# Column differences of the up weights: three units in four made ahead, the fourth made from its own loads

## The chip, the cores and the metric

The kernel runs on one core of a Trainium2 chip. The metric is the device time of one execution in microseconds; "before" is the median of three runs. Engines are named as in the profile: PE is TensorE's matmuls and PEld its weight loads, DVE is VectorE, ACT is ScalarE, POOL is GpSimd, SP is SyncE, which here does nothing but issue DMAs.

## The reference

One layer of a transformer block on x of 512 rows and 2048 columns, float32 throughout:

```python
h = rmsnorm(x, g_attn)
proj = h @ w_in                      # 2048 x 6152: q, k, v of 8 + 8 heads of 128, and 8 forget gates
o_sb = stick_breaking_attention(...) # 8 heads
o_fox = forgetting_attention(...)    # 8 heads
x = x + concat(head_rmsnorm(o_sb), head_rmsnorm(o_fox)) @ w_out
u = relu(rmsnorm(x, g_mlp) @ w_up)   # w_up: 2048 x 8192
x = x + (u * u) @ w_down             # w_down: 8192 x 2048
return rmsnorm(x, g_final)
```

## The kernel before

**Precision.** A float32 operand is split into a high part, cast on ACT (L63), and a low part, which DVE subtracts (L64). A plain product is then three matmuls (`mm3`, L95). The split tiles are `wh`, `wl` from a pool with three places each, and every fourth pair of the up stage comes from one more place and is called `wx`.

**Stages.** First the input projection and the attention of 16 heads (0 to some 590 us), then the output projection (to some 820 us), then the up product (to some 1477 us), then the down product, then the end. The change touches the first and the third.

**The up product** (class `Unit`). The 8192 columns of w_up are done in 32 units of 256 columns. Each unit is a 2 x 2 block product with seven products instead of eight: the rows of w_up in two interleaved halves, the columns in two blocks of 128, so a unit has blocks b11, b12, b21, b22 of 1024 x 128, 512 KB each. The seven products need, beside b11, b21 and b22, the differences

```
S1 = b12 - b11      product 5      (t1)
S3 = b22 - b12      product 7      (t3)
S2 = b22 - S1       product 6      (t2)
S4 = b21 - S2       product 4      made in the unit, L674
```

The sums of the rows' side (`F`, tiles `fh1` to `fh7` and `fl1` to `fl7`) are made once. A unit has three places of `rw` (five places of 8 KB per partition in all): one for b11 and t2, one for t1 and t3, one for b21 and b22, which come as one load of 1 MB (L646). Product p of the program order 1, (4 of the unit before), 5, 6, (3 of the unit before), 2, 7 takes 8 full-width matmuls with the high part (L678) and 8 half-width ones with the low part (L680). Products 1, 6, 7, 4 of a unit add up in one psum bank `psa`; ACT copies it out after 1, 6 and 7 as `s1`, `s6`, `s7` (L684), and each copy has to be done before the next of these products may write the bank. Products 5 and 3 use `psc`, product 2 `psb`.

**Stores between.** When a pair of units is done, the seven row-side sums of its 512 hidden columns are made for the down product (`store_form`, L708): DVE adds, ACT and DVE split into a tile `st`, and SP stores it in `ufd` in DRAM (L713). `st` has three places (tag `wraw`), so the cast of a set's fourth tile waits for the first store, and so on: the seventh waits for the fourth.

**Early sums.** S1, S3 and, for even units, S2 are made long before, among the projections of the first stage: `load_sums` reads b11, b12, b22 (three loads of 512 KB, L153) into a place that x used, two places in turn; DVE subtracts in place (L161, L162, L164); SP stores the result in `td` (L166). Odd units have only S1 and S3 made early, and make S2 in the unit, `b[6] = b[3] - b[5]` (L671), from b22 and S1. `drip` calls this along with the weight loads of `project_q`, 64 in number: at call n the sets up to 32 (n - 4) / 58 are done, each with the loads of the next set ahead of it.

**Order.** The order of each engine comes from a scheduler that runs its own timeline when the kernel is built; only PE's order in the first stage is written by hand. `tc.issue_after(i)` keeps what it covers behind instruction i. SP issues in its order: a DMA that waits for a place or for data holds all behind it.

## Time and profile before

| | |
|---|---|
| median of three runs | 2104.38 us (2103.6 to 2106.39) |
| the profiled execution | 2103.3 us, its span 2101.5 us |
| granted TensorE clock, mean | 0.995 |
| busy: PE, DVE, ACT | 98%, 76%, 51% of the span |
| moved by DMA | 464 MB, 221 GB/s |

The span is what the profiler saw from the first instruction to the last. Busy times of engines overlap, so they don't add up to the span. In the views below a row names the line, the engine, the operation and the tiles written and read (out<-in, numbers left out), and an arrow in brackets gives the idle time just before a row and what ended it. Rows of a timeline start with the time from the span's start and the duration. In windows each engine has its busy time and, in brackets, its instructions; then come the granted clock, the DMA engines' share and GB/s.

### The profile page before, as it was taken

How to read it: one execution, taken by the hardware profiler on the slowest of the kernel's cores; microseconds unless marked ns; L12 is line 12 of the kernel's file. 1: busy time of each engine (PE TensorE's matmuls, PEld its weight loads, DVE VectorE, ACT ScalarE, POOL GpSimd, SP SyncE). 2: the span in 40 equal slices, each digit the busy share in tenths (PEclk: the TensorE clock that was granted, in tenths of full speed). 3: DMA queues.
4: the chain of work that ended last, by engine and by line, in shares of the span. 5: the costliest groups of instructions: out<-in, count | busy, mean ns of one | idle time of the engine just before them, and what ended most of it. 6: DMA issues, size and time to landing. Idle time of an engine off the chain costs nothing.

```text
span 2101.5 us, 26836 instructions
## 1 busy us (share of the span) xinstructions
PE 2063.8 (98%) x10292; PEld 1753.2 (83%) x10292; DVE 1606.8 (76%) x1827; ACT 1064.9 (51%) x1426; POOL 64.9 (3%) x77
## 2 busy tenths in 40 slices
PE   9999999999999999999999999999999999999998
PEld 8888888888798888888888888888788888888886
DVE  5647757758766567777887888788788988988886
ACT  6334434444455565665665666566644444433433
POOL 0000000000110000000000000000000000000003
PEclk9999999999999999999999999999999999999999
DMA  7848958949963445566677576768867665764732
GB/s 240 288 120 265 325 171 292 347 118 293 316 211 110 151 140 171 187 229 236 228 243 237 198 247 230 240 209 275 314 203 260 240 223 177 261 235 145 259 122 80
DMA packets 358880, 464.27 MB, mean 221 GB/s; under 512 B 11696, under 2 KB 255456, under 8 KB 348640
## 3 DMA queue, kind: packets, MB, share of 16 engines
q1 hardware_dynamic: 357792, 460.44, 65.8%
q10 hardware_dynamic: 960, 2.13, 0.3%
q8 instruction: 81, 1.33, 0.2%
q14 instruction: 47, 0.39, 0.1%
HBM read 351.37 MB, written 111.15 MB: 220 GB/s over the span
## 4 chain that ended last, share of the span: by engine, by line
PE 81%; DMA 8%; DVE 5%; ACT 3%; issue 2%; SPq 0%; DVEq 0%; ACTq 0%
PE accd L96 8%; PE accd L98 8%; PE accd L97 8%; PE psa L678 7%; DMA ufd<-st 5%; PE accq L96 5%; PE accq L98 5%; PE accq L97 5%; PE psa L680 3%; PE psc L678 3%; PE acco L97 3%; PE acco L98 3%; PE acco L96 3%; PE accv L96 3%; PE accv L97 3%; PE accv L98 3%
## 5 line engine op out<-in xcount | busy, mean ns | idle before, releaser
L63 ACT CAST wh<-wraw 128x1024 fp32r<-128x1024 f32 (+2 forms) x133 | 135.4, 1019 | 178.8 <-PE accq L97 103.7
L63 ACT CAST wh<-wd 128x1024 fp32r<-128x1024 f32 (+1 forms) x136 | 135.0, 1000 | 178.9 <-PE accd L98 118.9
L64 DVE TENSOR_TENSOR wl<-wraw,wh 128x1024 fp32r<-128x1024 f32 (+2 forms) x133 | 158.0, 1188 | 75.9 <-ACT wh L63 75.6
L64 DVE TENSOR_TENSOR wl<-wu,wh 128x1024 fp32r<-128x1024 f32 x166 | 202.0, 1221 | 9.1 <-ACT wh L63 6.1
L96 PE MATMUL accq<-hH,wh 128*128 128x512 f32 x512 | 201.3, 393 | 0.0
L98 PE MATMUL accq<-hH,wl 128*128 128x512 f32 x512 | 200.1, 391 | 0.0
L97 PE MATMUL accq<-hL,wh 128*128 128x512 f32 x512 | 199.6, 390 | 0.0
L63 ACT CAST wh<-wu 128x1024 fp32r<-128x1024 f32 x166 | 172.1, 1047 | 46.1 <-issue 18.5
L64 DVE TENSOR_TENSOR wl<-wd,wh 128x1024 fp32r<-128x1024 f32 (+1 forms) x136 | 155.5, 1154 | 41.1 <-ACT wh L63 40.9
L96 PE MATMUL accd<-wh,uf 128*128 128x512 f32 x436 | 169.8, 389 | 2.6 <-DVE c L701 1.7
L98 PE MATMUL accd<-wh,uf 128*128 128x512 f32 x436 | 169.6, 389 | 0.0
L97 PE MATMUL accd<-wl,uf 128*128 128x512 f32 x436 | 169.6, 389 | 0.0
L63 ACT CAST wx<-wd 128x1024 fp32r<-128x1024 f32 (+1 forms) x88 | 87.5, 1000 | 123.1 <-PE accd L98 79.5
L678 PE MATMUL psa<-fh,wh 128*128 128x512 f32 x388 | 107.5, 399 | 14.2 <-ACT s L684 14.2
L64 DVE TENSOR_TENSOR wx<-wd,wx 128x1024 fp32r<-128x1024 f32 (+1 forms) x88 | 100.9, 1154 | 22.5 <-ACT wx L63 22.4
L98 PEld LDWEIGHTS accq<-hH,wl 128*128 128x128 f32 x512 | 96.1, 188 | 20.2
L97 PEld LDWEIGHTS accq<-hL,wh 128*128 128x128 f32 x512 | 96.4, 188 | 19.2
L96 PEld LDWEIGHTS accq<-hH,wh 128*128 128x128 f32 x512 | 96.4, 188 | 18.9
L96 PE MATMUL accd<-wx,uf 128*128 128x512 f32 x284 | 110.4, 389 | 0.1
L779 DVE TENSOR_TENSOR m<-m,accd 128x1024 f32<-128x1024 f32 x84 | 102.2, 1217 | 10.9 <-PE accd L98 10.8
L97 PE MATMUL accd<-wx,uf 128*128 128x512 f32 x284 | 110.5, 389 | 0.0
L98 PE MATMUL accd<-wx,uf 128*128 128x512 f32 x284 | 110.5, 389 | 0.0
(286 smaller groups left out, 4884.3 us busy)
## 6 DMA issues: line engine op xcount, KB each, us to landing
ufd<-st SPq DMA_DIRECT2D x98, 512.0 KB, 5.4
sums<-in_w_up_dram SPq DMA_DIRECT2D x96, 512.0 KB, 6.5
wd<-in_w_down_dram SPq DMA_DIRECT2D x48, 1024.0 KB, 6.8
wraw<-in_w_in_dram SPq DMA_DIRECT2D x84, 512.0 KB, 6.1
uf<-ufd SPq DMA_DIRECT2D x42, 1024.0 KB, 7.2
wu<-td SPq DMA_DIRECT2D x79, 512.0 KB, 5.0
wu<-in_w_up_dram SPq DMA_DIRECT2D x32, 1024.0 KB, 8.1
td<-sums SPq DMA_DIRECT2D x16, 1536.0 KB, 8.3
```

The source lines that it names most:

```text
L63: ins = casts[0] = act.copy(hi, src)
L64: lows[0] = dve.tensor_tensor(lo, src, hi.bitcast(F32), op=ALU.subtract)
L96: pe.matmul(out, sh, mh, start=first, stop=False, skip_group_check=True)
L97: pe.matmul(out, sh, ml, start=False, stop=False, skip_group_check=True)
L98: pe.matmul(out, sl, mh, start=False, stop=last, skip_group_check=True)
L678: pe.matmul(ps, hi[:, a, :], both, start=a == 0 and p in (1, 2, 5), stop=False, skip_group_check=True)
L680: pe.matmul(ps[:, :2 * P], lo[:, a, :], F[p][a // 4][:, a % 4, 0, :], start=False, stop=a == KC // 2 - 1, skip_group_check=True)
L779: dve.tensor_tensor(M[p][:, :, db, :], M[p][:, :, db, :], ps, op=ALU.add)
```

## The change

1. Units with u % 4 != 3 (24 of 32) get all three differences early, one set of three subtractions each, stored as one DMA. The odd units among them no longer make S2 themselves.
2. Units with u % 4 == 3 (8) get none early. They load b12 once and b22 twice more (L659 to L661: t1, t3, t2) and make S3 and S1 ahead of product 5 (L677, L678) and S2 ahead of product 6 (L680), all on DVE.
3. `drip` is written anew: at call n, 4n - 20 is divided by 9, and a remainder under 4 makes the set of that number, so a set every 2.25 calls. The loads of set i + 2 go out two calls after the store of set i, behind the weight load of that call. The first two sets' loads go out at call 2.

```diff
--- before.py
+++ after.py
@@ -56,7 +56,7 @@
     acc_cm = tc.tile_pool(name="acc", bufs=4, space=PSUM)
     acc = acc_cm.__enter__()
 
-    lows, casts = [None], [None]
+    lows, casts, loads = [None], [None], [None]
 
     def split(hi, lo, src, scale=None):
         if scale is None:
@@ -83,7 +83,7 @@
         src = src if isinstance(src, list) else [src]
         for i, r in enumerate(src):
             n = b // len(src)
-            sp.dma_start(raw[:, :, i * n:(i + 1) * n], r)
+            loads[0] = sp.dma_start(raw[:, :, i * n:(i + 1) * n], r)
         out = []
         per = min(a, 2 * NT // b)
         for i in range(0, a, per):
@@ -146,36 +146,36 @@
     td = [dp.tile([P, 3, KC // 2, P], F32, name=f"td{u}") for u in range(NU)]
     up_rows = w_up.rearrange("(a i p) f -> i p a f", i=2, p=P)
 
-    def load_sums(u):
-
-        r = mixp.tile([P, 3, KC // 2, P], F32, tag=f"x{u % 2}", name="sums")
+    def load_sums(u, i):
+
+        r = mixp.tile([P, 3, KC // 2, P], F32, tag=f"x{i % 2}", name="sums")
         for j, (i, c) in enumerate(((0, 2 * u), (0, 2 * u + 1), (1, 2 * u + 1))):
             sp.dma_start(r[:, j], up_rows[i][:, :, c * P:(c + 1) * P])
         return r
 
-    def up_sums():
-        r = load_sums(0)
-        for u in range(NU):
-            b11, b12, b22 = (r[:, j] for j in range(3))
-            now, r = r, load_sums(u + 1) if u + 1 < NU else None
+    early = [u for u in range(NU) if u % 4 != 3]
+    drops, raws, waiting = [0], {}, []
+
+    def drip(low, load):
+
+        drops[0] += 1
+        i, j = divmod(drops[0] * 4 - 20, 9)
+        with tc.issue_after(load.ins):
+            if drops[0] == 2:
+                raws.update((k, load_sums(early[k], k)) for k in range(2))
+            if waiting and (waiting[0][0] <= drops[0] or (j < 4 and waiting[0][1] == i)):
+                k = waiting.pop(0)[1]
+                raws[k] = load_sums(early[k], k)
+        if j > 3 or not 0 <= i < len(early):
+            return
+        b11, b12, b22 = (raws[i][:, j] for j in range(3))
+        with tc.issue_after(low.ins):
             dve.tensor_tensor(b11, b12, b11, op=ALU.subtract)
             dve.tensor_tensor(b12, b22, b12, op=ALU.subtract)
-            if u % 2 == 0:
-                dve.tensor_tensor(b22, b22, b11, op=ALU.subtract)
-            n = 2 if u % 2 else 3
-            yield sp.dma_start(td[u][:, :n], now[:, :n])
-
-    sums = up_sums()
-    drops = [0, 0]
-
-    def drip(ins):
-
-        drops[0] += 1
-        while drops[1] < min(NU, NU * (drops[0] - 4) // 58):
-            drops[1] += 1
-            with tc.issue_after(ins.ins):
-                next(sums)
-
+            dve.tensor_tensor(b22, b22, b11, op=ALU.subtract)
+        sp.dma_start(td[early[i]], raws.pop(i))
+        if i + 2 < len(early):
+            waiting.append((drops[0] + 2, i + 2))
 
     with (
         tc.tile_pool(name="hp", bufs=1) as hp,
@@ -260,7 +260,7 @@
             step = 8
             for k0 in range(0, KC, step):
                 w = load_w(w_in[k0 * P:(k0 + step) * P, c0:c0 + P].rearrange("(a p) c -> p a c", p=P), step, P)
-                drip(lows[0])
+                drip(lows[0], loads[0])
                 for i in range(step):
                     k = k0 + i
                     mm3(ps, *w[i], hH[:, k, :], hL[:, k, :], k == 0, k == KC - 1)
@@ -654,8 +654,14 @@
                 r, q = blocks(), blocks()
                 b11, t2, t1, t3 = r[:, 0], r[:, 1], q[:, 0], q[:, 1]
             sp.dma_start(b11, first[:, :, :P])
-            for t_, j in ((t1, 0), (t3, 1)) if u % 2 else ((t1, 0), (t2, 2), (t3, 1)):
-                sp.dma_start(t_, td[u][:, j])
+            self.raw = u not in early
+            if self.raw:
+                sp.dma_start(t1, first[:, :, P:])
+                sp.dma_start(t3, last[:, :, P:])
+                sp.dma_start(t2, last[:, :, P:])
+            else:
+                for t_, j in ((t1, 0), (t2, 2), (t3, 1)):
+                    sp.dma_start(t_, td[u][:, j])
             b21, b22 = wide(last)
             self.b = {1: b11, 5: t1, 6: t2, 2: b21, 7: t3, 3: b22, 4: b21}
             self.A, self.B, self.C = (ups.tile([P, NT], F32, tag=c, name=f"ps{c}") for c in "abc")
@@ -667,8 +673,11 @@
                 self.pair = hidden[0]
                 self.c = hidden[0][:, self.u % 2]
             hi, lo = (w.rearrange("p (a b) -> p a b", b=P) for w in hi_lo(2 * NT))
-            if p == 6 and self.u % 2:
-                dve.tensor_tensor(self.b[6], self.b[3], self.b[5], op=ALU.subtract)
+            if p == 5 and self.raw:
+                dve.tensor_tensor(self.b[7], self.b[7], self.b[5], op=ALU.subtract)
+                dve.tensor_tensor(self.b[5], self.b[5], self.b[1], op=ALU.subtract)
+            if p == 6 and self.raw:
+                dve.tensor_tensor(self.b[6], self.b[6], self.b[5], op=ALU.subtract)
             split(hi, lo, self.b[p])
             if p == 2:
                 dve.tensor_tensor(self.b[4], self.b[2], self.b[6], op=ALU.subtract)
```

What stands in the engines' order at the hand-over from unit 19 to unit 20, before and after. First SP's queue. The tiles `wu` are places of the units' operands, `td20` and `td21` the stored differences of units 20 and 21, `ufd` the stores of one set, the fourth of which is ufd6. Before:

```order
L713 DMA ufd1_14_6909<-st_10320 256x1x512
L713 DMA ufd4_14_6912<-st_10380 256x1x512
L658 DMA wu_10533<-td20_130 128x1024 x2
L713 DMA ufd5_14_6913<-st_10425 256x1x512
L646 DMA wu_10538<-in_w_up_dram 128x8x256
L656 DMA wu_10714<-in_w_up_dram 128x8x128
L713 DMA ufd6_14_6914<-st_10477 256x1x512
L713 DMA ufd2_14_6910<-st_10505 256x1x512
L713 DMA ufd7_14_6915<-st_10565 256x1x512
L713 DMA ufd3_14_6911<-st_10612 256x1x512
L658 DMA wu_10715<-td21_131 128x1024 x2
```

and now:

```order
L664 DMA wu_10500<-td20_130 128x1024 x2
L722 DMA ufd5_14_6865<-st_10392 256x1x512
L646 DMA wu_10505<-in_w_up_dram 128x8x256
L656 DMA wu_10681<-in_w_up_dram 128x8x128
L664 DMA wu_10681<-td21_131 128x1024
L722 DMA ufd6_14_6866<-st_10444 256x1x512
L722 DMA ufd2_14_6862<-st_10472 256x1x512
L722 DMA ufd7_14_6867<-st_10532 256x1x512
L664 DMA wu_10682<-td21_131 128x1024 x2
L722 DMA ufd3_14_6863<-st_10579 256x1x512
```

One more block, of td21, is read ahead of the fourth store (ufd6), and unit 21's other two now stand ahead of the seventh store (ufd3) and not behind it; one row carries both. In the pair before, unit 19's own t1 and t3 (L659, L660) stand at the place of that row, and its t2 (L661) at that of the single block.

Second ACT's order at the same place. `s6` and `s7` are the copies of unit 19's bank, `st` the casts of a set (the last one is the seventh), `c` the squares of relu; before:

```order
L63 CAST st_10477<-c_9931 128x512
L63 CAST st_10505<-c_9931 128x512
L63 CAST wh_10543<-wu_10532 128x1024
L684 COPY s6_10451<-psa_10355 128x512
L63 CAST st_10565<-c_9931 128x512
L63 CAST wh_10570<-wu_10353 128x1024
L63 CAST wh_10592<-wu_10533 128x1024
L705 ACTIVATE c_10297<-c_10297 128x1024
L63 CAST st_10612<-c_9931 128x512
L63 CAST wx_10617<-wu_10532 128x1024
L706 ACTIVATE c_10297<-c_10297 128x1024
L684 COPY s7_10528<-psa_10355 128x512
```

and now:

```order
L63 CAST st_10444<-c_9895 128x512
L63 CAST st_10472<-c_9895 128x512
L63 CAST st_10532<-c_9895 128x512
L63 CAST wh_10537<-wu_10318 128x1024
L63 CAST wh_10559<-wu_10500 128x1024
L693 COPY s6_10418<-psa_10320 128x512
L714 ACTIVATE c_10261<-c_10261 128x1024
L63 CAST wh_10605<-wu_10318 128x1024
L715 ACTIVATE c_10261<-c_10261 128x1024
L63 CAST st_10579<-c_9895 128x512
L63 CAST wh_10630<-wu_10505 128x1024
L693 COPY s7_10495<-psa_10320 128x512
```

The sixth cast moved ahead of s6, the seventh stands behind unit 19's product 3 (wh_10605), and between it and s7 there is now only the cast of unit 20's product 2 (wh_10630).

Third PE's order there. psa_10355 and psa_10320 are unit 19's bank before and now, psa_10540 and psa_10507 unit 20's; the digit of fh and fl is the number of the product. Before, from the middle of unit 19's product 7:

```order
L678 MATMUL psa_10355<-fl7_5711,wx_10509 128x512 x4
L680 MATMUL psa_10355<-fh7_5710,wx_10509 128x256 x4
L680 MATMUL psa_10355<-fl7_5711,wx_10509 128x256 x4
L678 MATMUL psa_10540<-fh1_5698,wh_10543 128x512 x4
L678 MATMUL psa_10540<-fl1_5699,wh_10543 128x512 x4
L680 MATMUL psa_10540<-fh1_5698,wl_10544 128x256 x4
L680 MATMUL psa_10540<-fl1_5699,wl_10544 128x256 x4
L678 MATMUL psc_10542<-fh5_5706,wh_10592 128x512 x4
L678 MATMUL psc_10542<-fl5_5707,wh_10592 128x512 x4
L680 MATMUL psc_10542<-fh5_5706,wl_10593 128x256 x4
L680 MATMUL psc_10542<-fl5_5707,wl_10593 128x256 x4
L678 MATMUL psa_10355<-fh4_5704,wh_10570 128x512 x4
```

and now, from unit 20's product 5:

```order
L687 MATMUL psc_10509<-fh5_5658,wh_10559 128x512 x4
L687 MATMUL psc_10509<-fl5_5659,wh_10559 128x512 x4
L687 MATMUL psa_10320<-fh7_5662,wx_10476 128x512 x4
L687 MATMUL psa_10320<-fl7_5663,wx_10476 128x512 x4
L689 MATMUL psa_10320<-fh7_5662,wx_10476 128x256 x4
L689 MATMUL psa_10320<-fl7_5663,wx_10476 128x256 x4
L689 MATMUL psc_10509<-fh5_5658,wl_10560 128x256 x4
L689 MATMUL psc_10509<-fl5_5659,wl_10560 128x256 x4
L687 MATMUL psb_10508<-fh2_5652,wh_10630 128x512 x4
L687 MATMUL psb_10508<-fl2_5653,wh_10630 128x512 x4
L687 MATMUL psa_10320<-fh4_5656,wh_10537 128x512 x4
L687 MATMUL psa_10320<-fl4_5657,wh_10537 128x512 x4
```

Unit 19's product 7 moved behind unit 20's product 1 and the high part of its product 5, and the high part of unit 20's product 2 moved ahead of unit 19's product 4.

## The prediction

> **What bounds the kernel now.** The page comes first, then the waits of PE, then PE in order of time, and then the engines around its longest stops. In the page's first part the columns are busy time, share and instructions; in the waits they are the total in us, how often, and the longest.
>
> ```profile
> span 2101.5 us, 26836 instructions
> PE 2063.8 (98%) x10292; PEld 1753.2 (83%) x10292; DVE 1606.8 (76%) x1827; ACT 1064.9 (51%) x1426; POOL 64.9 (3%) x77
> ...
> PE psa L678 <- ACT s L684: 15.3, 11, 3.4
> PE s L96 <- DVE pl L64: 3.1, 1, 3.1
> ```
>
> TensorE sets the time: only 38 us of the span are not matmuls. The matmuls stay as they are, so the change can win only from stops of PE, and lose only by new ones. Four tenths of the idle time is one kind: the up product's matmuls wait for ScalarE's copy of a psum bank. How long should that stage be? The pace of an undisturbed unit and the stage's first and last starts tell.
>
> ```profile
> 1238.95 1.10 PE L678 MATMUL psb<-fh,wh 128*128 128x512 f32 x4
> 1258.51 1.09 PE L678 MATMUL psb<-fh,wh 128*128 128x512 f32 x4
> ...
> L678 PE MATMUL psa<-fh,wh x388: 389/395/628, 819.5 to 1471.7; 128*128 128x512 f32 x194
> L678 PE MATMUL psc<-fl,wx x68: 388/389/395, 851.1 to 1475.5; 128*128 128x512 f32 x68
> ```
>
> Both psb rows are product 2, of units 20 and 21; between them lie the seven products of a unit: 19.56 us, 2.79 us each. 32 units make 625.9 us. The stage takes from 819.5 to about 1476.8 (the last start and the 1.3 us of low-half matmuls behind it), 657.3 us. So some 31 us are lost in it, of which I count the first 20 us and the hand-over at the end out: neither changes. Five stops carry most of the rest; the bracket is the idle time before the row.
>
> ```profile
> 983.09 1.35 PE L678 MATMUL psa<-fh,wh 128*128 128x512 f32 x4 [2.62 <-ACT s L684]
> 1065.00 1.34 PE L678 MATMUL psa<-fh,wh 128*128 128x512 f32 x4 [1.93 <-ACT s L684]
> 1310.18 1.19 PE L678 MATMUL psa<-fh,wh 128*128 128x512 f32 x4 [1.25 <-ACT s L684]
> 1392.64 1.32 PE L678 MATMUL psa<-fh,wh 128*128 128x512 f32 x4 [3.05 <-ACT s L684]
> ```
>
> With the one below they stand 82 us apart or a multiple of it: four units. Each falls where a unit u with u % 4 == 3 hands over to the next. This is the one at unit 19, all engines:
>
> ```profile
> 1214.01 0.38 SPq L646 DMA_DIRECT2D wu<-in_w_up_dram  x1
> 1215.15 0.38 SPq L656 DMA_DIRECT2D wu<-in_w_up_dram  x1
> 1215.75 12.03 SPq L713 DMA_DIRECT2D ufd<-st  x4
> 1225.90 0.62 ACT L63 CAST st<-c 128x512 fp32r<-128x512 f32 x1 [4.07 <-DMA ufd<-st]
> 1226.43 1.04 ACT L63 CAST wx<-wu 128x1024 fp32r<-128x1024 f32 x1
> 1228.33 0.56 ACT L684 COPY s<-psa 128x512 f32<-128x512 f32 x1
> 1228.95 1.44 PE L678 MATMUL psa<-fh,wh 128*128 128x512 f32 x4 [3.43 <-ACT s L684]
> 1233.40 1.08 PE L678 MATMUL psc<-fh,wh 128*128 128x512 f32 x4
> ```
>
> Read it upwards. PE stops because the copy s7 of unit 19 is late; s7 is late because the cast of the seventh store tile (1225.90) stands ahead of it in ScalarE's order and waits for the place that the fourth store frees. That store was issued at 1215.75 and landed 10 us later, behind 1.5 MB of loads issued just before it (unit 20's 1 MB, unit 21's first block). The whole chain from the cast to PE is 3.05 us.
>
> A stop costs more than its length. The product at 1228.95 takes 4.45 us to 1233.40 where 2.79 is normal: 1.66 us more. The windows' granted clock (the number ahead of the last two) says why:
>
> ```profile
> 985.00:988.00 3.00, 3.00 (x14) 2.64 (x12) 2.92 (x4) 1.72 (x3) 0.00 (x0) 0.60 0.53 128
> 1067.00:1070.00 3.00, 3.00 (x14) 2.71 (x13) 2.92 (x4) 1.72 (x3) 0.00 (x0) 0.62 0.53 134
> 1231.00:1234.00 3.00, 3.00 (x14) 2.69 (x13) 2.91 (x4) 1.69 (x3) 0.00 (x0) 0.64 0.56 142
> ```
>
> After the stops of 2.62, 1.93 and 3.43 us the clock was cut to some 0.6 on average over 3 us; I take the same 1.66 us behind 3.05, and none behind 1.25, whose first row (1.19) is nearly normal. So the five stops cost 12.3 us idle and 4 x 1.66 = 6.6 us of slow clock: 18.9 us. [...]
>
> Why is VectorE, and with it the load at 1214.01, so late there? Of the waits between 860 and 1480:
>
> ```profile
> ACT st L63 <- DMA ufd<-st: 60.3, 29, 4.2
> DVE wu L671 <- DMA wu<-in_w_up_dram: 57.8, 15, 5.7
> ...
> 1197.39 1.23 DVE L671 TENSOR_TENSOR wu<-wu 128x1024 f32<-128x1024 f32 x1 [5.71 <-DMA wu<-in_w_up_dram]
> ```
>
> In each odd unit L671 waits at the head of VectorE for the unit's 1 MB load, the last of its loads; all casts' low halves and sums queue behind it, and the loads that need their places.
>
> **The change part by part.** *L671 goes.* Units with u % 4 == 1 get the third difference ready made; their 57.8/15 = 3.85 us waits and one subtraction go. In u % 4 == 3 three subtractions on raw blocks replace the one:
>
> ```profile
> L674 DVE TENSOR_TENSOR wu<-wu 128x1024 f32<-128x1024 f32 x32 | 39.1, 1222 | 0.5
> ...
> 860.00:1480.00 620.00, 603.02 (x3396) 527.66 (x3395) 505.67 (x639) 381.03 (x501) 0.00 (x0) 0.99 0.70 235
> wu<-td SPq DMA_DIRECT2D x79, 512.0 KB, 5.0
> wu<-in_w_up_dram SPq DMA_DIRECT2D x31, 512.0 KB, 8.0
> ```
>
> A subtraction is 1.22 us. In the stage that is 8 x 2 more and 8 x 1 fewer, +9.8 us of VectorE, which is busy 505.7 of 620: hidden by the 57.8 us of waiting that go. The loads grow by one 512 KB block in each odd unit, 16 x 0.52 = 8.4 MB; at 235 GB/s for a share of 0.70, so 336 GB/s at full share, 1.56 us each, 25 us in all, and the share goes to about 0.74: hidden, but for the store behind such a block.
>
> *The long stops.* At unit 19 VectorE gains 5.71 us of wait and pays two subtractions, 2.44: it is 3.3 us ahead, and so is the 1 MB load, since its place comes free with the low half of unit 19's product 7. Ahead of the fourth store stands one more block, +1.56. So that store lands about 1.7 us sooner, near 1224.1 instead of 1225.8. What is needed also moves: by PE's order the products that it runs before it depends on the seventh cast are the same, only unit 19's product 7 now comes behind unit 20's first two, so it comes there again at 1225.5; but what it needs then is one cast of unit 20's product 2 behind the seventh, not two other instructions and s7: 0.62 + 1.04 less their overlap, 1.6 us instead of 3.05. The cast must start by 1223.9; it would by 1224.1. The stop of 3.43 us shrinks to a few tenths, too short for the clock. Over the eight such units I leave 0.4 us each, 3 us: this term is -16. Its bounds are -18.9 and, if the store is as late as now, 0.
>
> *The other stops* of that kind are 15.3 - 12.3 = 3.0 us, several of them behind L671; half goes, -1.5 (0 to -3).
>
> *The early stage.* Of 80 subtractions 8 go, of 96 loads 24, and a set's loads follow two weight loads later, after the store, not at the next set. Before, the queue stood in such loads:
>
> ```profile
> SPq L153 <- DMA td<-sums: 50.0, 19, 5.6
> ...
> 526.98 1.23 DVE L161 TENSOR_TENSOR sums<-sums 128x1024 f32<-128x1024 f32 x1 [1.16 <-DMA sums<-in_w_up_dram]
> 528.12 1.48 DVE L64 TENSOR_TENSOR pl<-pt,ph 128x1280 fp32r<-128x1280 f32 x1
> 529.66 0.53 PE L96 MATMUL s<-uh 128*128 128x512 f32 x1 [3.09 <-DVE pl L64]
> 520.00:540.00 20.00, 16.91 (x81) 14.33 (x80) 12.78 (x12) 8.84 (x10) 0.27 (x2) 0.91 1.06 350
> ```
>
> PE had only this one stop: pl stood behind subtractions, one of which waited 1.16 us for its load while the DMA share was 1.06. Their number ahead of pl is the same in the new order; the wait should go. Of 3.09 us and the 1.66 of the clock (0.91 over 20 us) I take -2.5; bounds 0 and -4.75. The 50 us of the queue gave PE nothing to wait for, so their end gives nothing.
>
> *What the new order of PE costs.* Some copies get less time: between product 6 and 7 of units 4k PE now has only 13 half-width matmuls for a copy of 0.56 us: a product's 2.79 us are eight full and eight half-width ones, so 2.79/24 = 0.116 each, 1.5 us. ScalarE has to be free then. No row shows this; from nothing to 0.8 us (a copy and half a cast late) at eight places, 0 to +6; I take +2, nearer to nothing since the copy fits nearly three times.
>
> Sum: -16 - 1.5 - 2.5 + 2 = -18. The profiled execution's 2103.3 becomes 2085.3; it stands 1.1 below the median of the three runs, so 2086.4, and I say 2086.
>
> **The rivals.** *A new wait at the raw subtraction, slower.* Unit 19's t1 and t3 are now read from the weights, and L677 and L678 need both; then follows the cast.
>
> ```profile
> 1186.93 0.83 SPq L658 DMA_DIRECT2D wu<-td  x2
> 1196.25 1.05 ACT L63 CAST wx<-wu 128x1024 fp32r<-128x1024 f32 x1 [2.46 <-issue]
> 1201.60 1.09 PE L678 MATMUL psc<-fh,wx 128*128 128x512 f32 x4
> ```
>
> Before they were issued at 1186.93 and landed 5.0 us later by the median, 1192. With the five VectorE instructions from L677 to L678 (5.6 us) and the cast's 1.05, product 5 could start at 1198.6, and PE wants it at 1201.6: 2.9 us of cover. But 512 KB from the weights took 8.0 us by the median where a block of td took 5.0, which would use the cover up just so. For it: that row. Against: the 8.0 belongs to loads behind a 1 MB load, and these two now stand behind stores. If they land 2.5 us beyond the cover, every fourth unit stops for 2.5 and pays 1.66: 8 x 4.16 = 33 us, on top of 2086 without the 3 that were left and the 2 of the copies: 2114. It decides from 23 us in all, 2.9 us at each place; a stop of 1.9 us, the shortest behind which the clock was cut, costs 3.6 with it.
>
> *The stop stays.* If L677 holds VectorE as long as L671 did, the 1 MB load is no sooner, and the fourth store is later by 1.56, which the shorter chain (1.4 us) just pays for. Then only the other stops and the early stage give: -4 + 2, 2102.
>
> *Half of it.* The store is only 1 us sooner: half of the 16 goes, 2094.
>
> [...]
>
> **How the numbers follow.** Forecast 0.62 (2086, its own range 2077 to 2092); half 0.10; the clock's other cause 0.02; the stop stays 0.13; the new wait 0.13. Below lie all bounds at their best, -18.9 - 3 - 4.75, 2077.7, so the range begins at 2076; it ends at 2104 with the stop that stays, and leaves out the new wait and a little more. 0.2% is 4.2 us, about what a measurement of this kernel can tell: faster holds the first three, 0.74; the stop that stays is within it, 0.13; slower 0.13.
>
> **What would show it.** Right: no wait of VectorE at the head of odd units beyond 1 us; no PE stop over 1.5 us between 900 and 1460, and windows there with a clock of 1.00; the seventh cast of a set waiting less than 1 us in units 4k; no stop near 529. Wrong: waits of DVE at L677 for DMA of over 3 us, PE stops every 78 us at product 5 or 2, or copies at product 6 of units 4k with stops of their own.

## The result and the profile after

The changed kernel takes 2080.44 us (median of four runs, 2078.39 to 2082.58) where the kernel before took 2103.99 beside it (2102.92 to 2106.39): a ratio of 0.9887, 95% interval 0.9869 to 0.9904. The forecast was 2086, in a range from 2076 to 2104. The profiled execution took 2080.91 us against 2103.3, so it stands for the medians.

The page of the changed kernel, its busy engines and the waits of PE in a view of their own (total us, how often, longest):

```profile
span 2079.2 us, 26762 instructions
PE 2055.9 (99%) x10292; PEld 1747.6 (84%) x10292; DVE 1601.8 (77%) x1827; ACT 1072.2 (52%) x1426; POOL 57.0 (3%) x77
```

```profile
PE accd L96 <- DVE c L710: 2.2, 1, 2.2
PE psa L687 <- DVE fl L64: 1.8, 1, 1.8
PE psa L687 <- ACT s L693: 1.6, 2, 1.4
PE s L96 <- DVE pl L64: 1.0, 1, 1.0
```

PE's waits for the copy out of `psa` have gone from 15.3 us in eleven places to 1.6 in two, and none of these lies before 1400 us. The wait of `accd` at the hand-over to the down stage has grown to 2.2 us, from 1.7 (its row of before is shown with the last unit, below). The up stage itself, the group with its first matmul (816.0 us),

```profile
L687 PE MATMUL psa<-fh,wh x388: 389/395/496, 816.0 to 1447.0; 128*128 128x512 f32 x194
```

and its last matmuls in order of time:

```profile
1451.89 0.64 PE L689 MATMUL psc<-fl,wx 128*128 128x256 f32 x4
```

It runs from 816.0 to 1452.5, 636.5 us instead of 657.3, and it starts 3.5 us sooner. A window over its middle shows the same. Its columns are the busy times of PE, PEld, DVE, ACT and POOL with their instructions, then the granted clock, the DMA share and GB/s; before first:

```profile
860.00:1440.00 580.00, 564.70 (x3182) 494.41 (x3181) 469.37 (x594) 355.60 (x467) 0.00 (x0) 0.99 0.70 232
```

```profile
860.00:1440.00 580.00, 579.11 (x3315) 509.57 (x3314) 495.43 (x631) 378.09 (x487) 0.00 (x0) 1.00 0.77 255
```

PE is busy for 579.1 of 580 us, at the full clock. VectorE (495.4 us for 469.4) and the DMA engines (a share of 0.77 for 0.70) are busier than before and, by these numbers, still have room. The account, by the profiled executions: early stage -3.5, up stage -20.8, everything behind it +2.0, in all -22.3 of the 22.4 by which the two differ.

The stop that the prediction read in detail was that at unit 19, 3.43 us. The same place after the change:

```profile
1194.29 0.38 SPq L646 DMA_DIRECT2D wu<-in_w_up_dram  x1
...
1199.77 0.38 SPq L656 DMA_DIRECT2D wu<-in_w_up_dram  x1
1200.21 0.57 SPq L664 DMA_DIRECT2D wu<-td  x1
1200.87 2.14 SPq L722 DMA_DIRECT2D ufd<-st  x3
1207.61 0.62 ACT L63 CAST st<-c 128x512 fp32r<-128x512 f32 x1 [1.35 <-DMA ufd<-st]
1208.14 1.05 ACT L63 CAST wh<-wu 128x1024 fp32r<-128x1024 f32 x1
1210.51 1.09 PE L687 MATMUL psb<-fh,wh 128*128 128x512 f32 x4
```

The 1 MB load (L646) is issued 6.6 us ahead of the fourth store (the first of the three at 1200.87); before it was 1.74 us. The store lands 6.7 us behind its issue, where it took 10.1. The seventh cast still waits for it, but 1.35 us, and the cast that PE needs behind it ends at 1209.2, 1.3 us before PE wants it (1210.51, no bracket, so no idle time). This cover differs from one execution to the next: in a second profile of the same kernel ("changed, again" below) the cast is late here, and PE stops:

```profile
1211.01 0.50 PE L687 MATMUL psb<-fh,wh 128*128 128x512 f32 x1 [1.16 <-ACT wh L63]
```

The waits of the stage between 860 and 1460 show the rival's place as well:

```profile
ACT st L63 <- DMA ufd<-st: 50.2, 23, 3.9
DVE wu L677 <- DMA wu<-in_w_up_dram: 5.8, 7, 1.7
```

The new head of VectorE in units 4k + 3 waits 1.7 us at most and 5.8 in all, where L671 waited 57.8. ScalarE's casts wait almost as much for stores as before (50.2 us for 60.3), but PE stops behind casts for 0.6 us in all.

### The profile page after: what moved, and what is told of

It reads as the page before. It is cut to its first block, busy times and chain, and to the rows that moved or that the text cites. A ratio compares the mean times of both kernels' runs of the same rounds, so it can differ in the third digit from the quotient of the medians.

```text
span 2079.2 us, 26762 instructions
## 1 busy us (share of the span) xinstructions
PE 2055.9 (99%) x10292; PEld 1747.6 (84%) x10292; DVE 1601.8 (77%) x1827; ACT 1072.2 (52%) x1426; POOL 57.0 (3%) x77
## 4 chain that ended last, share of the span: by engine, by line
PE 83%; DVE 7%; DMA 6%; issue 3%; ACT 1%; SPq 0%; DVEq 0%; ACTq 0%
PE accd L96 8%; PE accd L97 8%; PE accd L98 8%; PE psa L687 7%; PE accq L96 5%; PE accq L98 5%; PE accq L97 5%; PE psa L689 4%; PE psc L687 3%; DMA wu<-in_w_up_dram 3%; PE acco L97 3%; PE acco L98 3%; PE acco L96 3%; PE accv L96 3%; PE accv L97 2%
## 5 line engine op out<-in xcount | busy, mean ns | idle before, releaser
L687 PE MATMUL psa<-fl,wh 128*128 128x512 f32 x388 | 105.9, 391 | 1.8 <-DVE fl L64 1.8
```

What stands on the lines that cost most here:

```text
L687: pe.matmul(ps, hi[:, a, :], both, start=a == 0 and p in (1, 2, 5), stop=False, skip_group_check=True)
```

## The experiments

Each kernel was timed in the same sitting as the kernel before; the ratio is to that. All compute the whole output. "Up stage" is the span of its matmuls in the profile, "idle" a stop of PE in it.

| run | us | ratio, 95% interval | up stage, start and length |
|---|---|---|---|
| before | | | 819.5, 657.3 |
| changed | 2080.4 | 0.9887, 0.9869 to 0.9904 | 816.0, 636.5 |
| e1 loads only | 2106.6 | 1.0022, 1.0011 to 1.0032 | 822.1, 658.1 |
| e2 units only | 2082.0 | 0.9902, 0.9888 to 0.9917 | 817.1, 634.6 |
| e3 wait in 3 mod 4 | 2088.1 | 0.9929, 0.9914 to 0.9944 | 818.8, 643.9 |
| e4 wait in 1 mod 4 | 2086.3 | 0.9921, 0.9907 to 0.9936 | 813.8, 645.3 |
| e5 all early | 2082.8 | 0.9898, 0.9882 to 0.9914 | 823.4, 633.3 |
| e7 store, other queue | 2095.4 | 0.9949, 0.9931 to 0.9967 | 820.0, 652.7 |
| e8 all raw | 2126.0 | 1.0099, 1.0080 to 1.0118 | 814.8, 681.3 |
| e9 store ahead of load | 2084.6 | 0.9919, 0.9904 to 0.9933 | 821.4, 635.6 |
| e10 28 early | 2082.5 | 0.9908, 0.9893 to 0.9923 | 818.2, 638.5 |
| e6 last unit early | 2077.8 | 0.9872, 0.9856 to 0.9888 | 816.3, 635.9 |
| e6, again | 2076.3 | 0.9878, 0.9863 to 0.9893 | 816.4, 633.2 |
| changed, again | 2082.4 | 0.9908, 0.9891 to 0.9924 | 816.0, 638.5 |

**Which half of the change does it.** The change has two halves, where the early loads stand and which unit gets what. One kernel has only the first, one only the second.

Only the loads (base: changed):

```diff
-    early = [u for u in range(NU) if u % 4 != 3]
+    early = list(range(NU))
-        i, j = divmod(drops[0] * 4 - 20, 9)
+        i, j = divmod(drops[0] * 4 - 20, 7)
...
-            dve.tensor_tensor(b22, b22, b11, op=ALU.subtract)
+            if i % 2 == 0:
+                dve.tensor_tensor(b22, b22, b11, op=ALU.subtract)
...
+            if p == 6 and self.u % 2:
+                dve.tensor_tensor(self.b[6], self.b[3], self.b[5], op=ALU.subtract)
```

> Only the loads of the early sums are set as in the changed kernel; the units keep the old distribution (all 32 get sums early, odd units make the third difference in the up stage, behind their 1 MB load). Theory (the 1 MB load that VectorE waits for in odd units makes the fourth store late): the up stage keeps its long stops every fourth unit, 10 to 15 us idle and the slow clock behind each; only the early stop of 3.09 us goes: about 2100 us. Rival (it is where the early loads stand, or the new order that comes of it, that removed the stops): about 2082 us, the up stage as short as in the changed kernel, 636 us. If the early stop stays too, 2104.

Only the units (base: changed, with the loads and the stores of the sums placed as before):

```diff
+        r = load_sums(0)
+        for u in range(NE):
+            b11, b12, b22 = (r[:, j] for j in range(3))
+            now, r = r, load_sums(u + 1) if u + 1 < NE else None
...
+        while drops[1] < min(NE, NE * (drops[0] - 4) // 58):
```

> Only the distribution over the units is as in the changed kernel (24 units with three early differences, eight that subtract their own loads); the early loads stay where they were, each set's behind the sums of the set before. Theory: the up stage as short as in the changed kernel, 636 us instead of 657, and the early stop stays or changes by itself: 2080 to 2084 us. Rival (the position of the early loads did it): about 2100.

The first took 2106.6 us, a little slower than before; the second 2082.0, as the changed kernel. So the units carry it, and where the early loads stand gains nothing. I had put the early stop down to the loads, and that was wrong. The stop in the kernel with the loads alone, and in the one with the units alone:

```profile
528.86 1.23 DVE L174 TENSOR_TENSOR sums<-sums 128x1024 f32<-128x1024 f32 x1 [0.42 <-DMA sums<-in_w_up_dram]
530.00 1.48 DVE L64 TENSOR_TENSOR pl<-pt,ph 128x1280 fp32r<-128x1280 f32 x1
...
531.54 0.50 PE L96 MATMUL s<-uh 128*128 128x512 f32 x1 [3.12 <-DVE pl L64]
```

```profile
528.16 0.50 PE L96 MATMUL s<-uh 128*128 128x512 f32 x1 [1.04 <-DVE pl L64]
```

With the new loads and 32 sets pl is as late as ever (3.12 us); with the old loads and 24 sets the stop is 1.04 us, as it is in the changed kernel. The number of sets alone doesn't decide either. The next kernel, e3, also has 32 sets and the new loads, and there the wait for pl is short:

```profile
PE ssq L325 <- DVE pl L64: 0.5, 1, 0.5
```

In it no subtraction of the sums stands among the three VectorE instructions just ahead of pl; in the kernel with the loads alone two of the three just ahead are such subtractions, both waiting for their loads (0.26 and 0.42 us). So the stop goes by what the order puts ahead of pl, which comes out differently in each kernel.

**Which wait.** The change takes VectorE's wait for the 1 MB load out of two kinds of odd units. Two kernels put it back into one kind each, a third takes it out without any raw unit. All are the changed kernel with these edits.

Back in units 3 modulo 4 (32 sets, no raw unit):

```diff
-            dve.tensor_tensor(b22, b22, b11, op=ALU.subtract)
+            if early[i] % 4 != 3:
+                dve.tensor_tensor(b22, b22, b11, op=ALU.subtract)
...
+            if p == 6 and self.u % 4 == 3:
+                dve.tensor_tensor(self.b[6], self.b[3], self.b[5], op=ALU.subtract)
```

> The changed kernel, except that the units whose number is 3 modulo 4 again get two early differences and make the third behind their 1 MB load, as before; the units 1 modulo 4 keep all three early. Theory (the wait of VectorE in just these units delays the load and so the fourth store): the long stops come back, idle 8 to 12 us in four or five places with the slow clock behind them: 2093 to 2099 us. Rival (the order that comes with 24 early sets, or the waits in the other odd units, held the stops): they stay away, 2078 to 2084.

Back in units 1 modulo 4 (24 sets, units 3 modulo 4 raw):

```diff
-            dve.tensor_tensor(b22, b22, b11, op=ALU.subtract)
+            if early[i] % 4 != 1:
+                dve.tensor_tensor(b22, b22, b11, op=ALU.subtract)
...
+            if p == 6 and self.u % 4 == 1:
+                dve.tensor_tensor(self.b[6], self.b[3], self.b[5], op=ALU.subtract)
```

> The changed kernel, except that the units whose number is 1 modulo 4 get two early differences and make the third behind their 1 MB load; the units 3 modulo 4 subtract their own loads as in the changed kernel. Theory: no long stop comes back, only the short ones of these units, 0 to 3 us: 2080 to 2084 us. Rival (any such wait at the head of VectorE delays stores enough): long stops, 2090 or more.

All 32 early with three sums each:

```diff
-    early = [u for u in range(NU) if u % 4 != 3]
+    early = list(range(NU))
-        i, j = divmod(drops[0] * 4 - 20, 9)
+        i, j = divmod(drops[0] * 4 - 20, 7)
```

> All 32 units get their three differences early; no unit subtracts in the up stage but for the fourth block, and none waits for its 1 MB load there. Theory (that wait alone made the stops; the raw units are needed only to save early work): the up stage as short as in the changed kernel, 634 to 638 us, the early stage 0 to 6 us longer for its 8 more sets: 2080 to 2086 us. Rival (the raw units bring the gain by their own loads, which relieve the store queue): stops come back at every fourth unit, 2090 or more.

The last is the clearest. PE does not stop at all in its window:

```profile
860.00:1440.00 580.00, 580.00 (x3323) 510.39 (x3322) 472.16 (x607) 378.45 (x491) 0.00 (x0) 1.00 0.75 252
```

So the stops go with the wait, and the raw units are not needed for the up stage. PE runs unit 19's product 7 ahead of unit 20's product 5 here, as it did before the change, so the new order isn't needed for it either. VectorE also has 16 subtractions fewer in this stage; that this is not the reason shows in the changed kernel, where VectorE has more of them than before and the stops are gone too. Each of these edits makes the scheduler set the other engines' order anew, so no two of the kernels differ by the wait alone. What the raw units pay for is the early stage: with 32 sets the up stage starts at 823.4 instead of 816.0, a little more than expected, among other things by a new stop:

```profile
529.05 0.48 PE L300 MATMUL pt<-ident,w 128*128 128x128 f32 x1 [3.88 <-POOL w L292]
```

The other two fell between theory and rival. With the wait in units 3 modulo 4 the stops come back in four of the five old places, but lighter: PE waits 6.4 us for the copy where it waited 15.3, with two clock cuts instead of four. The stage is 7.4 us longer than in the changed kernel, not 12 to 19. At unit 19:

```profile
1204.80 0.38 SPq L648 DMA_DIRECT2D wu<-in_w_up_dram  x1
1205.93 0.38 SPq L658 DMA_DIRECT2D wu<-in_w_up_dram  x1
1206.37 2.73 SPq L666 DMA_DIRECT2D wu<-td  x1
1209.19 4.09 SPq L726 DMA_DIRECT2D ufd<-st  x3
...
1218.46 0.62 ACT L63 CAST st<-c 128x512 fp32r<-128x512 f32 x1 [3.81 <-DMA ufd<-st]
...
1219.62 0.80 PE L691 MATMUL psa<-fh,wh 128*128 128x512 f32 x1 [2.70 <-ACT s L697]
```

The chain is the old one, with a store that lands 9.2 us behind its issue. With the wait in units 1 modulo 4 I had expected up to 3 us and got an up stage 8.8 us longer: a stop in every fourth unit, now where the wait is. At unit 29:

```profile
1381.70 1.23 DVE L682 TENSOR_TENSOR wu<-wu 128x1024 f32<-128x1024 f32 x1 [4.09 <-DMA wu<-in_w_up_dram]
...
1396.71 0.52 SPq L726 DMA_DIRECT2D ufd<-st  x1
...
1408.13 0.62 ACT L63 CAST st<-c 128x512 fp32r<-128x512 f32 x1 [5.08 <-DMA ufd<-st]
...
1412.13 0.50 PE L691 MATMUL psa<-fh,wx 128*128 128x512 f32 x1 [1.75 <-ACT s L697]
```

Again a cast that waits for a store that was issued 11.4 us ago, and the copy behind it. So either kind of wait makes stops. One alone costs 7 to 9 us of stage against the changed kernel, both together 20.8. My view that the units 1 modulo 4 were nearly innocent, since few stops stood in them, was wrong. Whether the two really do more than add up is not shown: two profiles of one kernel differ by 2.0 and 2.7 us in this length (the repeated rows of the table), and against the kernel with all 32 early, which has as many sets, the wait in units 3 modulo 4 costs 10.6.

**The late store.** The prediction's chain has the store late because 1.5 MB of loads stand ahead of it. Two edits of the kernel before test that, the wait of VectorE staying in both. In the first the stores go by another queue:

```diff
-            sp.dma_start(ufd[g0][p][:, :, j0:j0 + 2, :], st.bitcast(F32))
+            pool.dma_start(ufd[g0][p][:, :, j0:j0 + 2, :], st.bitcast(F32))
```

> The kernel before, with the split stores of the up stage issued by GpSimd's queue instead of SyncE's. Theory (the fourth store of a set lands 10 us after its issue because it stands behind 1.5 MB of loads in one queue): it now lands in 3 to 5 us, the cast of the seventh store tile no longer waits there, and the long stops go as far as they do in the changed kernel: 2085 to 2092 us. Rival (the load that VectorE waits for is what is late, and the store only follows; or the transfers share the same engines and the queue does not matter): the stops stay, 2100 to 2106.

In the second the 1 MB load of the units 0 modulo 4 is issued behind the fourth store of the set (`fourth` holds that store):

```diff
-                sp.dma_start(raw, src)
+                if u % 4 == 0 and fourth:
+                    with tc.issue_after(fourth[0].ins):
+                        sp.dma_start(raw, src)
+                else:
+                    sp.dma_start(raw, src)
```

> The kernel before, with one edit: in the units 0 modulo 4 the 1 MB load is issued behind the fourth store of the set that is then being stored, not ahead of it; VectorE's wait at the third difference stays. Theory (what ends the long stops is that the fourth store of the set lands sooner, because less is under way ahead of it): the store lands in 5 to 7 us instead of 10, the long stops of the units 3 modulo 4 go, and the time falls by 12 to 18 us: 2086 to 2092. Rival (VectorE's own lateness behind its wait holds the copies, the store only follows): the store lands sooner and the stops stay, 2098 to 2106.

By the other queue the store at unit 19 is no faster. GpSimd issues the fourth and fifth at 1212.44, and the cast that waits for the fourth starts 10.0 us later:

```profile
1212.44 1.41 POOL L713 DMA_DIRECT2D ufd<-st  x2 [4.38 <-DVE st L64]
...
1222.48 0.62 ACT L63 CAST st<-c 128x512 fp32r<-128x512 f32 x1 [3.39 <-DMA ufd<-st]
...
1224.58 0.50 PE L678 MATMUL psa<-fh,wh 128*128 128x512 f32 x1 [2.71 <-ACT s L684]
```

The time still fell, to 2095.4 (six runs, 2089.57 to 2097.70), neither what the theory nor what the rival had said: PE waits 12.9 us for copies instead of 15.3, and the four clock cuts of the up stage are gone but for a new one at its end, behind 1.84 us at 1468 (why is below). Leaving SP's queue therefore doesn't help this store. It does change the order of landing: the 512 KB block that SP issued at 1211.46, 1.0 us ahead of the store, lands 3.2 us behind it. In the kernel before none of 44 stores that had such loads under way ahead of them landed before one of them; by GpSimd's queue 20 of 65 did (of the stores whose landing the traces have). But the 1 MB load, issued 2.1 us ahead, is still ahead of it, and with that much under way the store takes its 10 us all the same. The second edit changes what is under way:

```profile
1204.59 0.52 SPq L719 DMA_DIRECT2D ufd<-st  x1
1205.16 0.60 SPq L650 DMA_DIRECT2D wu<-in_w_up_dram  x1
...
1208.50 0.62 ACT L63 CAST st<-c 128x512 fp32r<-128x512 f32 x1 [0.19 <-DMA ufd<-st]
...
1216.35 0.86 PE L684 MATMUL psa<-fh,wh 128*128 128x512 f32 x3
```

Ahead of these, VectorE at the third difference of unit 19:

```profile
1186.23 1.23 DVE L677 TENSOR_TENSOR wu<-wu 128x1024 f32<-128x1024 f32 x1 [2.15 <-DMA wu<-in_w_up_dram]
```

With the load behind it the store is done 3.9 us after its issue, the cast waits 0.19 us, and it stands 7.9 us ahead of the matmul that stopped before (1216.35, now without idle time). The up stage is 635.6 us, as short as in the changed kernel, with none of the early sums touched; PE waits for copies twice in it, 2.9 us in all. This bears the chain out: at unit 19 PE runs its products in the old order, and VectorE still waits 2.15 us for its load. One thing qualifies it. The scheduler made a new order of the other engines from the edit, and VectorE's waits for the loads in the window fell by themselves, from 55.7 to 22.3 us. At unit 19 this brings the store's issue forward by about 2 us; the other 6 us are its landing.

**What a raw unit costs.** All units subtract their own loads, no early sums at all:

```diff
-    early = [u for u in range(NU) if u % 4 != 3]
+    early = []
```

> No early sums at all: every unit subtracts its own loads, three subtractions more in the up stage for each, and the early stage has no sums, loads or stores. Theory (raw subtractions are hidden as long as VectorE has room, and it has 505 of 620 us busy before): VectorE gets 2.44 us more in each of the 24 other units and is close to full, 19.6 us a unit of which about 18 busy; small stops in each unit, 2080 to 2095 us. Rival (a raw unit waits for its loads and stops PE): 1 us or more in each unit, 2100 or more. Second rival (raw costs nothing): 2074 to 2079, as the early stage gets shorter.

```profile
860.00:1440.00 580.00, 555.85 (x3111) 484.44 (x3110) 532.72 (x651) 349.43 (x454) 0.00 (x0) 0.98 0.74 237
```

2126.0 us. The stage is 681.3 us, 44.8 longer than in the changed kernel for 24 more raw units, 1.9 us each. VectorE is busy for 532.7 of 580 us and PE waits for copies 26.6 us in 20 places. VectorE's wait for its own loads (L677) is 7.9 us in this window, which points to the room on VectorE and not to the loads, though which link comes last there was not followed. One raw unit in four is nearly free (636.5 us of stage against 633.3 with all early); all raw are not. The early stage gains only 1.2 us from having no sums, so 24 sets are cheap there.

**The last unit.** The stop that the change made longer lies at the hand-over to the down stage. Before:

```profile
1478.48 0.50 PE L96 MATMUL accd<-wh,uf 128*128 128x512 f32 x1 [1.68 <-DVE c L701]
```

The granted clock stayed at 1.00 behind it. In the changed kernel there is a stop ahead of it too, at the copy of the last unit:

```profile
1446.16 1.19 PE L687 MATMUL psa<-fh,wh 128*128 128x512 f32 x4 [1.40 <-ACT s L693]
...
1454.74 0.50 PE L96 MATMUL accd<-wh,uf 128*128 128x512 f32 x1 [2.21 <-DVE c L710]
```

The windows around the second row:

```profile
1451.70:1455.10 3.40, 1.19 (x9) 0.94 (x9) 3.40 (x5) 1.56 (x2) 0.00 (x0) 1.00 1.05 395
1455.10:1458.50 3.40, 3.40 (x10) 2.63 (x9) 3.40 (x6) 0.51 (x1) 0.00 (x0) 0.51 1.04 420
```

VectorE (the third busy time) works all through both windows, and its late sum (L710) stops PE for 2.21 us, 0.5 more than before; the clock is halved behind it, where it was not before. Unit 31, the last, is a raw one. One set more takes its three subtractions away:

```diff
-    early = [u for u in range(NU) if u % 4 != 3]
+    early = [u for u in range(NU) if u % 4 != 3 or u == NU - 1]
```

> The changed kernel with one set more: unit 31, the last, gets its sums early too. Theory (the new stop at the hand-over to the down stage, 2.2 us idle and 3.4 us of slow clock, comes from VectorE's late copies behind the last unit's own subtractions): the stop goes or falls under 1.8 us, and 2 to 4 us with it: 2076 to 2079 us. Rival (it comes from the order at the hand-over itself): no change, 2079 to 2082.

2077.8 us, with 0.47 us left of that stop and no cut. Since this is a difference of 3 us between two sittings, it was timed again beside the changed kernel, with one more distribution, 28 units early:

```diff
-    early = [u for u in range(NU) if u % 4 != 3]
+    early = [u for u in range(NU) if u % 8 != 3]
-        i, j = divmod(drops[0] * 4 - 20, 9)
+        i, j = divmod(drops[0] * 4 - 20, 8)
```

> The kernel with the last unit early too, timed again beside the changed kernel on the same chip: 1 to 4 us below it, about 2078 us; if the difference of the first timing came from the chips, no difference.

> The changed kernel itself, timed again on the same chip as the two before: 2080 to 2082 us, 0.987 to 0.990 of the kernel before.

> The changed kernel with 28 units early and only each eighth unit (3 modulo 8) on its own loads. Theory (the up stage has no stops with 24 or 32 early sets alike, and the early stage loses time by the number of sets): between the changed kernel and the one with all 32, 2078 to 2083 us, the up stage 633 to 637 us, and no stop at the hand-over as the last unit is early; if the early stop stays at about 1 us, down to 2075.

The kernel with the last unit early took 2075.62 to 2076.66 us in four runs, the changed kernel 2080.82 to 2084.47, so it is 6 us better. The hand-over, first in the changed kernel and then with the last unit early:

```profile
1456.72 0.50 PE L96 MATMUL accd<-wh,uf 128*128 128x512 f32 x1 [2.21 <-DVE c L710]
```

```profile
1450.12 0.50 PE L96 MATMUL accd<-wh,uf 128*128 128x512 f32 x1 [0.48 <-DVE c L710]
```

Between the two profiled spans are 7.0 us (2081.2 and 2074.2). Behind the up stage lie 2.1 of them: 1.7 of idle time here and as much for the clock cut that goes with it, less 1.3 for a new stop at 1459.85. The stage itself is 5.3 us shorter: 1.8 in the stops of the last unit's own products and 2.1 in stops of 0.5 to 1.2 us further up, which the changed kernel had in this profile and hardly in the first; the rest I did not place. The stage starts 0.4 us later. With 28 sets the time is that of the changed kernel, 2082.5: the up stage starts 2 us later, has stops of 0.3 to 1.2 us at six places, and a clock cut at 823.7, behind a wait of 1.77 us near its start that nearly all these kernels have and only this one pays for (why is below). The best of what was tried is 25 sets, one in four units raw but for the last.

## Why the prediction was right, and where its steps were off

**The long stops, -16, and the other stops, -1.5.** Right in mechanism, mis-sized. Idle time and clock cuts of that kind went from 21.9 us (15.3 and 4 x 1.66) to 1.6; the stage shows -20.8 where the two terms had -17.5. I had left 0.4 us at each of eight places because the store seemed to come just 0.2 us late. In this profile the cast is 2.9 us ahead of PE's need (1207.61 against 1210.51) where it was 0.4 behind, a shift of 3.3 us where I had 1.7. The piece that I under-sized is the load: it moved 4.7 us against PE's need (from 11.5 to 16.2 us ahead of it), not 3.3. The store itself is issued as far ahead of the need as before (9.8 and 9.6 us) and lands 3.4 us sooner. I had taken the load's 3.3 us less 1.56 for one more block ahead of the store. What the next product needs does come where it was put, 1.6 us behind the cast's start. Why the load gained 1.4 us more than VectorE's own sum is not shown, and no run prices the block's 1.56 us by itself: the rows show only that the store lands sooner with the block ahead of it, the 1 MB load now being 6.6 us ahead. The size is also less firm than one profile makes it look. The stops behind casts, which stand where I had left 3 us, are 0.6 us in the first profile and 2.4 in the second (1.16, 0.52 and 0.71), whose stage is 18.8 us shorter than before.

**The early stop, -2.5.** The size was near, -3.5, and the cause was wrong in part. I wrote that the number of subtractions ahead of pl stays and the wait for the load goes. The wait of 1.16 us did go, but the number fell too: behind the last `qf` ahead of pl stood four subtractions, and three in the changed kernel. The new loads don't bring this: the kernel with them alone keeps the stop, and the one with fewer sets alone loses it.

**Tighter copies, +2.** Nothing of it: no stop is at a copy at product 6 in either profile. The two stops behind casts in the first (0.31 and 0.25 us) are at product 2.

**What was not in the sum, +2.0.** The hand-over. I had counted it out as unchanged, and the last unit is a raw one: its subtractions fall into the stretch where VectorE has no room. The stop there grew from 1.68 to 2.21 us, and most of the 2.0 is the clock, which was halved only behind the longer one. A reader of the diff could have asked which of the eight raw units stands last.

**The rivals.** The new wait at L677 had to cost 2.9 us at each place to matter; VectorE waits there 1.7 us at most, within the cover, since t1 and t3 land 4.9 and 6.3 us behind their issue by the median, where 8.0 would have used the cover up. The stop that stays did not come, since the load was sooner and VectorE was not held. The clock's other cause, which has 0.02 in the chances, is shown by no run: between 860 and 1440, where before a cut stood behind each stop of 1.93 us and more, none is left, and the granted clock is 1.00.

**The clock.** The prediction charged 1.66 us behind stops of 1.93 us and more and nothing behind shorter ones, which is close but leaves out where a stop falls. In the clock records of the kernel before, the five halved stretches ahead of the very end last 3.413 us each, and the later four begin 133, 157, 205 and 253 times 3.4133 us behind the first, within 0.002 us; in the changed kernel the one at 1455.1 also lasts 3.413 us, and that at the very end begins 181 times 3.4133 us behind it. So in these traces the cuts stand on a fixed raster. Here are stretches of the raster with the stretch behind, from the kernel before, from that with the wait in units 1 modulo 4 and from that with the store in the other queue; PE's busy time is the first after the length, and the granted clock the one after POOL:

```profile
1062.50:1065.90 3.40, 1.47 (x9) 1.13 (x9) 2.80 (x4) 3.40 (x6) 0.00 (x0) 1.00 0.46 178
1065.90:1069.30 3.40, 3.40 (x13) 2.91 (x12) 3.37 (x4) 2.47 (x3) 0.00 (x0) 0.50 0.29 51
```

```profile
1011.90:1015.30 3.40, 1.61 (x9) 1.19 (x8) 2.76 (x3) 3.40 (x5) 0.00 (x0) 1.00 0.87 335
1015.30:1018.70 3.40, 3.40 (x14) 3.02 (x13) 2.18 (x3) 1.90 (x4) 0.00 (x0) 0.50 0.99 292
```

```profile
1219.70:1223.10 3.40, 2.17 (x14) 1.75 (x12) 0.65 (x1) 0.62 (x2) 0.00 (x0) 1.00 0.88 349
1223.10:1226.50 3.40, 1.92 (x8) 1.61 (x9) 2.60 (x4) 3.40 (x5) 0.69 (x1) 1.00 0.41 165
1226.50:1229.90 3.40, 3.40 (x20) 2.95 (x19) 3.37 (x4) 1.62 (x3) 0.00 (x0) 1.00 0.60 188
```

A stretch in which PE is busy 1.47 or 1.61 us is followed by one at half speed (0.50). The last three rows are the stop of 2.71 us in the kernel with the other queue: it is longer than those two, but the raster cuts it into parts of 1.2 and 1.5 us, and the clock stays at 1.00. In the traces of the kernel before and of the changed one, the start and the end of each left out, no stretch at full speed with up to 1.68 us of idle time was followed by a cut, and each with 1.93 us and more was. The row with 1.61 us busy, 1.79 idle, lies between them and has its cut. At 1.77 us of idle time it went both ways, first in the kernel with 28 units early, then in that with the other queue:

```profile
820.30:823.70 3.40, 1.63 (x8) 1.04 (x7) 3.40 (x6) 3.40 (x9) 0.00 (x0) 1.00 0.90 263
823.70:827.10 3.40, 3.40 (x16) 3.21 (x16) 3.30 (x9) 3.34 (x9) 0.00 (x0) 0.50 1.11 380
```

```profile
1383.60:1387.00 3.40, 1.63 (x8) 1.30 (x8) 2.26 (x4) 3.40 (x5) 0.69 (x1) 1.00 0.45 178
1387.00:1390.40 3.40, 3.40 (x20) 2.94 (x19) 3.37 (x4) 1.97 (x4) 0.00 (x0) 1.00 0.63 199
```

So in these rows the change from no cut to a cut lies near 1.77 us of idle time, 0.52 of 3.413.

## What to carry to other kernels

When PE waits for a small copy, follow the copy's engine back past the copy: here a cast three store tiles on was held by a store (4.07 us at unit 19), the store by loads that were issued just ahead of it (it landed after 10.1 us), and these by an unrelated wait of VectorE (5.71 us). This chain could be cut at its cheapest link: the 1 MB load set behind one store brought 2084.6 us with no work moved. And when one unit in four is to carry extra work, ask which of these is the last one, and what the engine does there.

## What the runs showed of the hardware that was not expected

A 512 KB store that was issued just behind 1.5 MB of loads landed after 10 us at unit 19, by the same queue (10.1) or by GpSimd's (10.0) alike; the same store issued ahead of them landed in 3.9. By GpSimd's queue 20 of 65 stores landed ahead of a load that SP had issued before them, which none of 44 did by SP's own in the kernel before; at this place that gained nothing.

What a stop of PE cost besides its length went by where it fell in the raster of 3.413 us: one of 2.71 us, in two parts of 1.2 and 1.5, left the clock behind it at 1.00; a stretch with 1.79 us idle was followed by one at 0.50.
